# A decoder step on one core: main products that read and write from the last column to the first, with every second column of a slab as weights

## The chip, the cores and the metric

The kernel runs on one core of a Trainium2 chip. The metric is the time of one execution on the device, in microseconds; lower is better. TensorE multiplies: a product first loads a block of 128 x 128 weights (LDWEIGHTS) and then streams the columns of the moving operand through it (MATMUL), and the sums are written to PSUM. VectorE (DVE), ScalarE (ACT) and GpSimd (POOL) do the elementwise work, and SyncE (SP) issues the DMAs.

## The reference

One layer of a decoder with three parallel branches, on 256 prompt tokens and 8 x 4 sample tokens, 288 in all, in float32:

```python
h = rms_norm(x, p['g_mix'])
proj = h @ p['w_in']
u_lin, u_gate, q_sb, k_sb, v_sb, q_mem, gate_logits = jnp.split(proj, SPLIT_POINTS, axis=-1)
...                                   # y_conv: GLU, causal depthwise conv, LayerNorm, swish, projection
...                                   # y_sb: stick-breaking attention over paged keys and values
...                                   # y_mem: softmax attention into 256 memory tokens
gates = jax.nn.sigmoid((gate_logits + p['b_gate']).astype(jnp.float32)).astype(x.dtype)
merged = gates[:, :, 0] * y_conv + gates[:, :, 1] * y_sb + gates[:, :, 2] * y_mem
x = x + merged @ p['w_o']
h2 = rms_norm(x, p['g_mlp'])
x = x + jnp.square(jax.nn.relu(h2 @ p['w_up'])) @ p['w_down']
```

The model is 2048 wide and the MLP 8192. The large products (`w_in`, the three branch projections, `w_o`, `w_up`, `w_down`) hold nearly all of the arithmetic. The outputs are also the new keys and values, the last rows of the convolution's input, and the memory's keys and values.

## The kernel before

**Layout.** Activations lie with the features on the 128 partitions and the 288 tokens along the columns, so one product of a 128 x 128 block of weights with a tile of 288 columns gives 128 output features of all tokens. Weights are the loaded (stationary) operand, activations the moving one.

**Slabs.** All weights stand in one array `wall` of 504 slabs, each 128 partitions x 1024 words, put in order of use on the host in `_layout`. A main slab holds 8 blocks of 128 columns next to each other: `put` lays down the blocks of 1024 input rows for one tile of 128 outputs; `put_pair` lays 4 times two adjacent output tiles; `put_rows` lays two pieces of 512 columns. The first 16 slabs are for the memory's keys and values (L541), where the slab is the moving operand; the other 488 are weights of main products.

**Two parts for each number.** Each slab comes by DMA into a "wr" tile. ScalarE (L305) rounds it to float32r, the high part "wh", and VectorE (L316) takes the difference, the low part "wl". Activations are kept as a high and a low part as well. A product with full precision is three products: high weights with the high and with the low activation, and low weights with the high activation. So each main slab feeds 24 products. The tiles of the parts have small leads ahead of their data: weights of main slabs begin 5 words into their tile (`SHIFT`), the activations 4 or 36 words into theirs (`AHEAD`, `HOME`), 320 words apart (`APART`).

**The products.** `chunk` (L486 to L488) issues a list of products into one PSUM accumulation. `products` makes the list from one slab, the 16 with high weights first and then the 8 with low weights, in pieces of 6; `main_tile` does two slabs (2048 input rows) into one bank of PSUM and passes the sum on. `conv_products` does the first four tiles of `w_in` with its own list, and calls `chunk` too. The other matrix products (attention, sums of squares, transposes) issue their own instructions at other lines.

**Order.** The order of instructions on each engine is written by a planner (`Order`): each job is a generator that yields what it needs next (engine, estimated time, flags, buffers), and the planner always takes the one that can start first. A main product is entered with the estimate `MM` = 0.131 us.

Of the kernel before, what the change touches and what calls it, by code (L numbers as in the profile page):

```python
# [14 lines left out]
P = 128  # L15
D_MODEL = 2048
KT = D_MODEL // P
# [19 lines left out]
N_SLABS = 504  # L37
# [37 lines left out]
class Order:  # L75
# [15 lines left out]
    def add(self, gen, rank, at=None):  # L91
        job = Job(gen, rank, self.now.ready if at is None and self.now else at or 0.0)
        self.jobs.append(job)
        was, self.now = self.now, job
        self.step(job)
        self.now = was
# [10 lines left out]
    def give(self, pool, n=1):  # L107
        self.pools[pool] += [self.now.ready] * n
# [57 lines left out]
def pe(us, *flags, **take):  # L166
    return Ask("PE", us, flags, **take)
# [16 lines left out]
def tile_decoder_step(ctx: ExitStack, tc: tile.TileContext, xT, memT, wall, cvec, kmat, ptab,  # L184
                      kpool, vpool, mkc, mvc, hist,
                      yT, oK, oV, oCp, oCs, oMK, oMV):
    nc = tc.nc
# [24 lines left out]
    def bank(p):  # L212
        return tl(p, [P, 512])
# [107 lines left out]
    def start_slab(s):  # L321
        at_slab[:] = [s, order.now.ready]
# [10 lines left out]
    hm, hx = [None] * KT, [None] * KT  # L333
# [149 lines left out]
        done(rm_done)  # L483


    def chunk(ps, todo, first, last):  # L486
        for i, (w, a) in enumerate(todo):
            nc.tensor.matmul(ps, w, a, start=(first and i == 0), stop=(last and i == len(todo) - 1))  # L488

    slab_no = [0]  # L490
    FULL = [k * P for k in range(8)]
# [2 lines left out]
    def products(ps, uses, acts, first=True, last=True, n=T):  # L494

        s = slab_no[0] - 1
        sl = slabs[s]
        high = [(sl.h, c, a, x) for c, a in zip(uses, acts) for x in (0, 1)]
        low = [(sl.l, c, a, 0) for c, a in zip(uses, acts)]
        todo = high + low  # L500
        for i in range(0, len(todo), STEP):
            part = todo[i:i + STEP]
            yield pe(len(part) * MM, *sl.split, *{a.flag for _, _, a, _ in part})
            if i == 0 and first:
                start_slab(s)
            chunk(ps, [(w[:, c:c + P], a.l if x else a.h) for w, c, a, x in part],
                  first and i == 0, last and i + STEP >= len(todo))

    def main_tile(acts, evac, rank=1.0, n_slabs=2):
        yield pe(0.0, pm=1)  # L510
        ps = bank("pm")[:, :T]
        for i in range(n_slabs):
            slab_no[0] += 1
            yield from products(ps, FULL, acts[8 * i:8 * i + 8], i == 0, i == n_slabs - 1)
            give("w")
        add(evac(ps), rank)
# [33 lines left out]
    def conv_products(evacs):  # L550

        s0 = slab_no[0]
        slab_no[0] += KT // 2
        yield pe(0.0, pa=2)
        ps = [bank("pa")[:, :T], bank("pa")[:, :T]]
        lead = 3
        turns = [(k2, o) for k2 in range(lead) for o in (0, 1)] + [(k2, o) for k2 in range(lead) for o in (2, 3)]
        turns += [(k2, o) for k2 in range(lead, KT // 2) for o in range(4)]
        for k2, o in turns:
            s = s0 + k2  # L560
            sl = slabs[s]
            if len(ps) <= o:
                yield pe(0.0, pm=1)
                ps.append(bank("pm")[:, :T])
            todo = []
            for i in range(2):
                w = slice(i * 512 + o * P, i * 512 + (o + 1) * P)
                todo += [(sl.h, w, "h", 2 * k2 + i), (sl.h, w, "l", 2 * k2 + i)]
            for i in range(2):
                todo.append((sl.l, slice(i * 512 + o * P, i * 512 + (o + 1) * P), "h", 2 * k2 + i))  # L570
            yield pe(6 * MM, *sl.split, hx_in[2 * k2], hx_in[2 * k2 + 1])
            if o == 0:
                start_slab(s)
            chunk(ps[o], [(w[:, c], getattr(hx[k], x)) for w, c, x, k in todo], k2 == 0, k2 == KT // 2 - 1)
            if k2 == KT // 2 - 1:
                add(evacs[o](ps[o]), 1.0 + 0.01 * o)
            if o == 3:
                give("w")
        for k in range(KT):
            hx[k].flag = hx_in[k]  # L580
# [806 lines left out]
    def branch_products(br, acts):  # L1387
        for j0 in range(0, KT, 4):
            for j in range(j0, j0 + 4):
                yield from main_tile(hx, gate(br, j))  # L1390
            for j in range(j0, j0 + 4):
                if br == 1:
                    yield from main_tile(acts, branch(br, j), 1.0, 1)
                    continue
                yield pe(0.0, pm=1)
                ps = bank("pm")[:, :T]
                if j % 2 == 0:
                    slab_no[0] += 1
                yield from products(ps, [k * 2 * P + (j % 2) * P for k in range(4)], acts)
                if j % 2:  # L1400
                    give("w")
                add(branch(br, j)(ps), 1.0)
# [10 lines left out]
    def main():  # L1413
        yield from warm_up()
        yield from mem_products()
        yield from conv_products([evac_lin(0, "pa"), evac_gat(0, "pa"), evac_lin(1, "pm"), evac_gat(1, "pm")])
        for j in range(2, CT):
            yield from main_tile(hx, evac_lin(j, "pm"))
# [62 lines left out]
def _layout(inp):  # L1481
    import numpy as np

    a = {k: np.asarray(v) for k, v in inp.items()}
# [8 lines left out]
    x = np.concatenate([a["x_prompt"][0], a["x_sample"].reshape(NS, D_MODEL)], 0)  # L1493

    wall = np.empty((N_SLABS, P, SLAB), np.float32)
    at = [0]

    def put(w, j, r0=0, rows=D_MODEL):
        for half in range(rows // 1024):
            blk = w[r0 + half * 1024:r0 + (half + 1) * 1024, j * P:(j + 1) * P]  # L1500
            wall[at[0]].reshape(P, 8, P)[:] = blk.reshape(8, P, P).transpose(1, 0, 2)
            at[0] += 1
# [40 lines left out]
    for c in range(4):  # L1543
        for f in range(KT):
            put(a["w_up"][0], c * KT + f)
        for j in range(KT):
            put(a["w_down"][0], j, c * D_MODEL)
    assert at[0] == N_SLABS

    cvec = np.zeros((P, NCV), np.float32)  # L1550
    cvec[:, C_GMIX:C_GMIX + KT] = cols(a["g_mix"][0])
# [15 lines left out]
    i = np.arange(P)  # L1567
# [3 lines left out]
    r, c = i[:, None] % NS, np.arange(NS)[None, :]  # L1571
# [49 lines left out]
```

## Time and profile before

| | |
|---|---|
| time, median of 3 runs | 1634.39 us (1634.28 to 1634.63) |
| span of the profiled execution | 1632.5 us |
| the median less that span | 1.9 us |
| TensorE busy | 1627.7 us, 12,786 products |
| weight loads busy | 1610.3 us, 12,786 loads |
| DVE, ACT, POOL busy | 992.1, 739.3, 139.1 us |
| read from memory | 297.05 MB, 186 GB/s over the span with what is written |

For the profiled execution the span, from its first to its last instruction, is what is recorded as its own time. Products are pipelined: the duration of one goes from its issue to the drained end and overlaps the next, so the busy time of TensorE doesn't tell what a product costs; the distance from one start to the next does. Weight loads (PEld) overlap the products.

### The profile page before, as it was taken

Reading aid. Unit: us, or ns where it says so; the run is one execution under the profiler, and the core shown is the slowest. Engines: PE = TensorE matmul, PEld = TensorE weight load, DVE = VectorE, ACT = ScalarE, POOL = GpSimd, SP = SyncE. Lnnn points to the kernel's source line nnn. Section 1 sums busy time; section 2 is a strip of 40 time slices with the busy share of each in tenths; the row PEclk is TensorE's granted clock in tenths of the full one; section 3 lists DMA queues with packets and bytes.
Section 4 is the critical chain, followed back from the end, with each engine's and each line's share of the span. In section 5 each row is a group of like instructions: output and inputs, shape, how many; then the busy total and the mean of one; then the engine's idle time right before and its main releaser. Section 6 shows DMA issues by size and latency. Waiting matters only on the chain.

```text
span 1632.5 us, 30962 instructions
## 1 busy us (share of the span) xinstructions
PE 1627.7 (100%) x12786; PEld 1610.3 (99%) x12786; DVE 992.1 (61%) x1471; ACT 739.3 (45%) x1070; POOL 139.1 (9%) x104
## 2 busy tenths in 40 slices
PE   9999999999999999999999999999999999999999
PEld 7999999999999999999999999999999999999999
DVE  8889888877677655565555544455445554455443
ACT  8746766644444534444443333333333333333332
POOL 0020000000000000001222200121001210022100
PEclk9999999999999999999999999999999999999999
DMA  9787465777755555546655555555555555555563
GB/s 339 217 186 251 153 209 189 248 257 252 254 166 169 163 179 167 174 153 212 191 176 168 169 168 168 169 169 174 165 173 170 168 170 169 168 168 168 180 194 99
DMA packets 107103, 305.39 MB, mean 187 GB/s; under 512 B 19922, under 2 KB 29522, under 8 KB 106962
## 3 DMA queue, kind: packets, MB, share of 16 engines
q1 hardware_dynamic: 106818, 303.39, 58.2%
q8 instruction: 100, 1.64, 0.4%
q14 instruction: 41, 0.34, 0.1%
q10 hardware_dynamic: 144, 0.02, 0.0%
HBM read 297.05 MB, written 6.32 MB: 186 GB/s over the span
## 4 chain that ended last, share of the span: by engine, by line
PE 99%; DMA 0%; SPq 0%; ACT 0%; DVE 0%; issue 0%
PE pm L488 93%; PE pm L541 3%; PE pa L488 1%; PE pl L1017 1%; PE pl L1190 0%; PE pa L854 0%; PE pa L855 0%; PE pa L853 0%; DMA wr<-in_wall 0%; PE pl L1033 0%; PE pa L827 0%; PE pa L1144 0%; PE pa L908 0%; PE pa L1141 0%; PE pa L1143 0%; PE pa L1107 0%
## 5 line engine op out<-in xcount | busy, mean ns | idle before, releaser
L305 ACT CAST wh<-wr 128x1024 fp32r<-128x1024 f32 (+1 forms) x520 | 530.3, 1022 | 648.1 <-PE pm L488 597.0
L488 PE MATMUL pm<-a,wh 128*128 128x288 f32 x5184 | 739.1, 293 | 0.0
L316 DVE TENSOR_TENSOR wl<-wr,wh 128x1024 fp32r<-128x1024 f32 (+1 forms) x520 | 617.2, 1190 | 195.2 <-ACT wh L305 190.5
L488 PEld LDWEIGHTS pm<-a,wh 128*128 128x128 f32 x5184 | 696.7, 188 | 1.3 <-issue 1.2
L488 PE MATMUL pm<-a,wl 128*128 128x288 f32 x2592 | 397.0, 292 | 0.0
L488 PEld LDWEIGHTS pm<-a,wl 128*128 128x128 f32 x2592 | 358.4, 188 | 0.0
L488 PE MATMUL pm<-k,wh 128*128 128x288 f32 x2160 | 306.7, 292 | 0.0
L488 PEld LDWEIGHTS pm<-k,wh 128*128 128x128 f32 x2160 | 290.2, 188 | 0.0
L488 PE MATMUL pm<-k,wl 128*128 128x288 f32 x1120 | 171.6, 292 | 0.0
L488 PEld LDWEIGHTS pm<-k,wl 128*128 128x128 f32 x1120 | 155.1, 188 | 0.0
L1346 POOL TENSOR_TENSOR t<-t 128x288 f32<-128x288 f32 x64 | 96.7, 1511 | 599.5 <-DVE t L1343 599.5
L1360 DVE TENSOR_TENSOR a<-a,pm 128x288 f32<-128x288 f32 x64 | 29.0, 454 | 122.4 <-PE pm L488 122.4
L1343 DVE SCALAR_TENSOR_TENSOR t<-pm,rx 128x288 f32<-128x288 f32 x64 | 29.2, 457 | 90.4 <-PE pm L488 90.4
L1349 ACT CAST k<-t 128x288 fp32r<-128x288 f32 x56 | 24.1, 433 | 115.6 <-POOL t L1346 115.6
L1262 DVE TENSOR_TENSOR t<-pm,rx 128x288 f32<-128x288 f32 x48 | 22.0, 458 | 71.5 <-PE pm L488 71.5
L488 PE MATMUL pm<-s,wh 128*128 128x288 f32 x400 | 65.1, 292 | 0.0
L719 DVE SCALAR_TENSOR_TENSOR a<-a,cv,a 128x256 f32<-128x256 f32 x120 | 57.5, 480 | 1.4
L1332 POOL TENSOR_TENSOR t<-t,t 128x288 f32<-128x288 f32 x15 | 21.6, 1441 | 419.3 <-ACT t L1329 419.3
L488 PEld LDWEIGHTS pm<-s,wh 128*128 128x128 f32 x400 | 56.6, 188 | 0.0
L1351 DVE TENSOR_TENSOR k<-t,k 128x288 fp32r<-128x288 f32 x52 | 23.8, 458 | 51.1 <-ACT k L1349 51.1
L541 PE MATMUL pm<-wh,a 128*128 128x512 f32 x128 | 34.6, 391 | 0.2 <-ACT wh L305 0.2
L488 PE MATMUL pm<-s,wl 128*128 128x288 f32 x160 | 33.8, 292 | 0.0
(212 smaller groups left out, 784.4 us busy)
## 6 DMA issues: line engine op xcount, KB each, us to landing
wr<-in_wall SPq DMA_DIRECT2D x488, 512.0 KB, 3.6
wr<-in_wall SPq DMA_DIRECT2D x32, 256.0 KB, 4.8
k<-in_kpool SPq DMA_DIRECT2D x32, 256.0 KB, 5.9
k<-in_vpool SPq DMA_DIRECT2D x32, 256.0 KB, 5.8
k<-in_mkc SPq DMA_DIRECT2D x8, 512.0 KB, 10.2
k<-in_mvc SPq DMA_DIRECT2D x8, 512.0 KB, 6.5
t<-in_xT SPq DMA_DIRECT2D x16, 144.0 KB, 3.7
out_yT<-a SPq DMA_DIRECT2D x16, 144.0 KB, 1.9
```

The source lines that it names most:

```text
L305: nc.scalar.copy(sl.h[:, c], sl.raw[:, c])
L316: nc.vector.tensor_sub(sl.l[:, c], sl.raw[:, c], sl.h[:, c].bitcast(F32))
L488: nc.tensor.matmul(ps, w, a, start=(first and i == 0), stop=(last and i == len(todo) - 1))
L541: nc.tensor.matmul(ps[m], y[:, m * P:(m + 1) * P], z[:, w], start=(k == 0 and j < 2), stop=(k == KT - 1 and j in (4, 5)))
L719: nc.vector.scalar_tensor_tensor(c[:, :NP], up[:, k:k + NP], w, c[:, :NP], op0=ALU.mult, op1=ALU.add)
L1262: nc.vector.tensor_mul(g, ps, rx)
L1332: nc.gpsimd.tensor_add(sq_sum[0], sq_sum[0], res[0])
L1343: nc.vector.scalar_tensor_tensor(r, ps, 0.0, r2, op0=ALU.max, op1=ALU.mult)
L1346: nc.gpsimd.tensor_mul(r, r, r)
L1349: nc.scalar.copy(a.h, r)
L1351: nc.vector.tensor_sub(a.l, r, a.h.bitcast(F32))
L1360: nc.vector.tensor_add(x1[j], x1[j], ps)
```

## The change

In `chunk`, the moving operand is read from its last column to its first, and the sums are written to PSUM from the last column to the first, so that each sum lands where it did. The weights of a block are no longer 128 adjacent words of the slab but every second word of a pair of blocks (256 words): `block` gives the first, third, fifth ... word for the even block of the pair and the second, fourth ... for the odd one. The host lays the slabs out to match, from slab 16 on. The 16 memory slabs and all other matrix products are as before.

```diff
+    def block(w, c):
+
+        pair = w[:, c // (2 * P) * 2 * P:(c // (2 * P) + 1) * 2 * P]
+        return pair.rearrange("p (c two) -> p two c", two=2)[:, c // P % 2]
+
     def chunk(ps, todo, first, last):
         for i, (w, a) in enumerate(todo):
-            nc.tensor.matmul(ps, w, a, start=(first and i == 0), stop=(last and i == len(todo) - 1))
+            nc.tensor.matmul(ps[:, ::-1], w, a[:, ::-1], start=(first and i == 0), stop=(last and i == len(todo) - 1))
...
-            chunk(ps, [(w[:, c:c + P], a.l if x else a.h) for w, c, a, x in part],
+            chunk(ps, [(block(w, c), a.l if x else a.h) for w, c, a, x in part],
                   first and i == 0, last and i + STEP >= len(todo))
...
-            chunk(ps[o], [(w[:, c], getattr(hx[k], x)) for w, c, x, k in todo], k2 == 0, k2 == KT // 2 - 1)
+            chunk(ps[o], [(block(w, c.start), getattr(hx[k], x)) for w, c, x, k in todo], k2 == 0, k2 == KT // 2 - 1)
...
     assert at[0] == N_SLABS
+    for s in range(KT, N_SLABS):
+        v = wall[s].reshape(P, 4, P, 2)
+        v[:] = wall[s].reshape(P, 4, 2, P).transpose(0, 1, 3, 2).copy()
```

## The prediction

> **What bounds the kernel now.** I read the busy shares of the page first, then its chain that ended last, then the TensorE clock row.
>
> ```profile
> PE 1627.7 (100%) x12786; PEld 1610.3 (99%) x12786; DVE 992.1 (61%) x1471; ACT 739.3 (45%) x1070; POOL 139.1 (9%) x104
> ...
> PEclk9999999999999999999999999999999999999999
> ...
> PE 99%; DMA 0%; SPq 0%; ACT 0%; DVE 0%; issue 0%
> PE pm L488 93%; PE pm L541 3%; PE pa L488 1%; PE pl L1017 1%; PE pl L1190 0%; PE pa L854 0%; PE pa L855 0%; PE pa L853 0%; DMA wr<-in_wall 0%; PE pl L1033 0%; PE pa L827 0%; PE pa L1144 0%; PE pa L908 0%; PE pa L1141 0%; PE pa L1143 0%; PE pa L1107 0%
> ```
>
> TensorE is never idle for long, its clock is not cut, and 93 + 1 hundredths of the span are the products of L488, the only instructions of the program that the diff touches. So the change is worth what it does to the time from one L488 product to the next, and nothing else. How many there are, the instructions of that line tell (forms of the tiles that they read):
>
> ```profile
> L488 PE MATMUL pm<-a,wh x5184: 289/292/401, 54.0 to 1528.1; 128*128 128x288 f32 x200
> L488 PE MATMUL pm<-a,wl x2592: 289/292/383, 54.6 to 1529.2; 128*128 128x288 f32 x200
> L488 PE MATMUL pm<-k,wh x2160: 290/290/294, 730.3 to 1627.3; 128*128 128x288 f32 x197
> L488 PE MATMUL pm<-k,wl x1120: 290/292/294, 732.4 to 1628.7; 128*128 128x288 f32 x187
> L488 PE MATMUL pm<-s,wh x400: 290/294/294, 734.8 to 1628.0; 128*128 128x288 f32 x134
> L488 PE MATMUL pm<-s,wl x160: 290/290/294, 736.3 to 1629.0; 128*128 128x288 f32 x160
> L488 PE MATMUL pa<-a,wh x64: 290/292/382, 48.9 to 72.8; 128*128 128x288 f32 x64
> L488 PE MATMUL pa<-a,wl x32: 290/293/298, 49.4 to 73.1; 128*128 128x288 f32 x32
> ```
>
> The sum of the counts is 11,712. The duration of one (292 ns) is from its issue to its drained end and overlaps the next, so it is not what one costs. The cost is the distance of starts, which the chain in order of time gives, since it merges unbroken stretches (start, length, what, count):
>
> ```profile
> 541.70 297.18 PE pm L488 x2286
> 839.15 790.15 PE pm L488 x6078
> ```
>
> 790.15 us over 6078 products is 130.0 ns each, and 297.18 over 2286 is 130.0 too. So 11,712 x 130.0 ns = 1522.6 us of the 1632.5 us span are set by this one number. The rest, about 110 us, is the memory products of L541, the attention and convolution products, and the edges; the change leaves it alone. The profiled execution spans 1632.5 us; the median of the runs is 1634.39, so 1.9 us lie around the span, and I add them to every span below.
>
> **What of the 130 ns is streaming.** Products of other widths are priced in the same way, in the timeline of TensorE (start, length, what, count):
>
> ```profile
> 40.75 1.07 PE L541 MATMUL pm<-wh,a 128*128 128x512 f32 x4
> 41.65 0.61 PE L541 MATMUL pm<-wl,a 128*128 128x512 f32 x2
> 42.11 1.07 PE L541 MATMUL pm<-wh,a 128*128 128x512 f32 x4
> ...
> 128.80 0.28 PE L853 MATMUL pa<-a,a 128*128 128x256 f32 x1
> 128.92 0.28 PE L854 MATMUL pa<-a,a 128*128 128x256 f32 x1
> 129.03 0.28 PE L855 MATMUL pa<-a,a 128*128 128x256 f32 x1
> 129.16 0.28 PE L853 MATMUL pa<-a,a 128*128 128x256 f32 x1
> 129.28 0.28 PE L854 MATMUL pa<-a,a 128*128 128x256 f32 x1
> 129.40 0.28 PE L855 MATMUL pa<-a,a 128*128 128x256 f32 x1
> 129.51 2.25 PE L488 MATMUL pm<-a,wh 128*128 128x288 f32 x16
> ```
>
> Six products of 512 columns take 42.11 - 40.75 = 1.36 us, 226.7 ns each. Six of 256 columns take 129.51 - 128.80 = 0.71 us, 118.3 ns each. So a further column costs (226.7 - 118.3) / 256 = 0.423 ns, and 118.3 - 256 x 0.423 = 10 ns of each product are no streaming. A product of 288 columns streams for 288 x 0.423 = 121.9 ns, and 8.1 of the 130.0 ns are extra. With the slope between 288 and 512 columns instead, (226.7 - 130.0) / 224 = 0.432, streaming is 124.3 ns and 5.7 ns are extra. So 5.7 to 8.1 ns of each main product can be won at most: 67 to 95 us in all.
>
> Is that extra fixed? Two rows say that it depends on where the operands lie. By the line through 256 and 512 columns, 288 columns would cost 121.9 + 10 = 131.9 ns; those products read tiles without the leads AHEAD and SHIFT, and the main products, which have them, cost 130.0. And after the sum of squares, whose moving tile (a "t" tile) has no lead either, the next main product starts later than 130:
>
> ```profile
> 132.64 0.30 PE L827 MATMUL pa<-t,ones_r 128*128 128x288 f32 x1
> 132.78 2.26 PE L488 MATMUL pm<-a,wh 128*128 128x288 f32 x16
> ```
>
> That is 0.14 us for the same 288 columns on an engine with nothing to wait for (to a hundredth, so a weak witness alone). During each product the weights of the next are read from the same memory. I take the extra to be, mostly, these two reads getting in each other's way.
>
> [...]
>
> **The change part by part.** The number of products, of weight loads, of DMAs and of their bytes stays as it is, and so do the casts (L305) and subtractions (L316), which handle whole slabs; the shuffle of the slabs is done on the host, outside the time. The 16 memory slabs keep their layout. No wait is added, and the planner's order is the same, since MM and the asks are the same. Cost of all that: 0.
>
> *Moving columns last to first* (a[:, ::-1]): the same 288 adjacent words of 4 bytes, from the other end. No row shows such a read. [...] *Sums written last to first* (ps[:, ::-1]): the same words of the bank; no row shows it. Nearest is the forward write, 0; I take 0, and as an upper bound I keep one extra more, 8.1 ns.
>
> *Weights from every second column*: one load now walks over 1,024 bytes of a partition instead of 512. What a load costs by itself is seen where the products are short (weight loads, start and length):
>
> ```profile
> 176.10 0.19 PEld L1143 LDWEIGHTS pa<-s,ones_r 128*128 128x128 f32 x1
> 176.21 0.19 PEld L1144 LDWEIGHTS pa<-s,tri_r 128*128 128x128 f32 x1
> 176.32 0.36 PEld L488 LDWEIGHTS pm<-a,wh 128*128 128x128 f32 x2
> ```
>
> Loads follow each other at 0.11 us for 128 columns, 0.86 ns a column. So a load hides under a product of 0.130 us with 0.020 us to spare: it may become 18% longer for nothing. Bounds: 0 if a load at a step of two costs what it does now; 0.22 - 0.13 = +0.09 us for each product if it takes twice as long. I take 0. [...]
>
> *Both together*: now the product walks 4 bytes in 0.423 ns, 9.5 bytes/ns, and the load 4 bytes in 0.86 ns, 4.7 bytes/ns. [...] With a step of two the load walks 8 bytes in 0.86 ns, 9.3 bytes/ns: the same speed as the product, within the accuracy of the rows. If both also walk the same way, their distance stays what it is at the start, and a collision that holds one of them up shifts it out of the way of the next. Then most of the extra goes. The diff turns the product's way round; which way the load walks through its tile no row shows. Here I choose: the same way. Of the 5.7 to 8.1 ns I take 6.0, near the lower end, because some turn-around between products will remain, which these rows can't separate. Sum: 11,712 x 6.0 ns = 70.3 us; span 1632.5 - 70.3 = 1562.2; with 1.9, **1564.1 us**, at 124.0 ns a product.
>
> What would be late next: a slab feeds 24 products, 3.12 us now and 2.98 then. The stretches (PE, PEld, DVE, ACT, POOL busy; clock; DMA share) of the early and the late part:
>
> ```profile
> 200.00:300.00 100.00, 100.00 (x871) 99.24 (x870) 84.42 (x166) 66.58 (x135) 0.96 (x1) 1.00 0.64 225
> 1100.00:1200.00 100.00, 100.00 (x772) 100.00 (x771) 48.09 (x55) 35.61 (x38) 8.67 (x6) 1.00 0.54 170
> ```
>
> Late, DVE at 48% and ACT at 36% have room for a pace 5% higher. Early, DVE at 84% would go to some 88%; I cost this at nothing. If that cover is gone, the gain of the products outside the two long stretches is lost: 11,712 less 8,364 are 3,348, at 6.0 ns 20 us.
>
> **The rivals.** [...]
>
> *B: the load itself becomes the bound.* It decides once a load at a step of two lasts over 0.130 us. At twice the time, 0.22, the sum is 11,712 x 0.09 = +1054 us, 2688 us. [...]
>
> *C: nothing changes.* The extra is a turn-around inside TensorE, or the mirrored read and the mirrored write come to the engine as what they were, and the step of two hides in the 0.020 us. For it: the extra hardly varies, 130.0 in both long stretches. Against: the 1.9 ns and the 0.14 us. Time: 1634.4.
>
> **How the numbers follow.** Forecast 0.60, A 0.26, C 0.08, B 0.06. A measurement of this kernel can tell about 0.2% from no change, 3.3 us, or 0.28 ns a product. So faster 0.60, same 0.08, slower 0.32. The forecast's own range is from the whole extra gone (1634.4 - 95 = 1539) to a third of it (2 ns, 23 us: 1611). The range of the whole must take in C and a good part of A: up to 1700, which leaves out B and about 0.08 of A at the top, and a few hundredths below 1539. So 1539 to 1700.
>
> **What would show it.** Right: the long unbroken stretch of L488 at about 124 ns a product, L541 still at 227, weight loads still 0.19 us from issue to end, DVE's late share up to about 50%. If the step of two slows the load, that duration grows, and above all its distance of starts. [...] Early waits of L488 on L316 or L305 would show that the supply eats part of the gain. Wrong altogether: a distance of 130.0 as before, or over it.

## The result: 44 us slower

The changed kernel takes 1678.89 us (median of 4 runs, 1678.87 to 1679.38), the kernel before 1634.51 us beside it: 44.4 us more, a ratio of 1.0272 (95% interval 1.0257 to 1.0286). The prediction was 1564.1 us; the measured time lies in the stated range, on the other side of no change.

The page of the changed kernel first (`chunk` now issues at L493, the memory products are L546):

```profile
span 1677.6 us, 30962 instructions
...
PE 1672.9 (100%) x12786; PEld 1655.3 (99%) x12786; DVE 993.3 (59%) x1471; ACT 740.2 (44%) x1070; POOL 139.2 (8%) x104
...
PEclk9999999999999999999999999999999999999999
```

The work of DVE, ACT and POOL is what it was, TensorE is still busy throughout at an uncut clock (1.0 granted), and the span is 45.1 us longer. Its chain in order of time (start, length, what, count) has the same unbroken stretches:

```profile
555.68 306.32 PE pm L493 x2286
862.27 812.09 PE pm L493 x6078
```

812.09 us over 6078 products is 133.6 ns each, and 306.32 over 2286 is 134.0, where both were 130.0. 11,712 products at 3.6 to 4.0 ns more are 42 to 47 us: nearly the whole loss, beside about 1 us ahead of the first main product. The weight loads of that line (duration min/median/max in ns), before and after, show one thing more:

```profile
L488 PEld LDWEIGHTS pm<-a,wh x5184: 186/188/215, 53.9 to 1528.0; 128*128 128x128 f32 x200
```

```profile
L493 PEld LDWEIGHTS pm<-a,wh x5184: 192/196/220, 55.1 to 1570.2; 128*128 128x128 f32 x200
```

A weight load, from issue to end, had a median of 188 ns and now has 196. So the load did get longer, but by 8 ns, within the 20 ns that the prediction had found to spare.

### The profile page after: what moved, and what is told of

It is laid out like the page before. It is cut to its first block, busy times and chain, and to the rows that moved or that the text cites. A ratio compares the mean times of both kernels' runs of the same rounds, so it can differ in the third digit from the quotient of the medians.

```text
span 1677.6 us, 30962 instructions
## 1 busy us (share of the span) xinstructions
PE 1672.9 (100%) x12786; PEld 1655.3 (99%) x12786; DVE 993.3 (59%) x1471; ACT 740.2 (44%) x1070; POOL 139.2 (8%) x104
## 4 chain that ended last, share of the span: by engine, by line
PE 99%; DMA 0%; SPq 0%; ACT 0%; issue 0%; DVE 0%
PE pm L493 93%; PE pm L546 2%; PE pa L493 1%; PE pl L1022 1%; PE pl L1195 0%; DMA wr<-in_wall 0%; PE pa L859 0%; PE pa L860 0%; PE pa L858 0%; PE pl L1038 0%; PE pa L832 0%; PE pa L1149 0%; PE pa L913 0%; SPq L283 0%; PE pa L1146 0%; SPq L396 0%
## 5 line engine op out<-in xcount | busy, mean ns | idle before, releaser
L493 PE MATMUL pm<-a,wh 128*128 128x288 f32 x5184 | 756.2, 297 | 0.0
L493 PEld LDWEIGHTS pm<-a,wh 128*128 128x128 f32 x5184 | 717.2, 197 | 1.3 <-issue 1.2
L493 PE MATMUL pm<-a,wl 128*128 128x288 f32 x2592 | 410.7, 299 | 0.0
L493 PEld LDWEIGHTS pm<-a,wl 128*128 128x128 f32 x2592 | 371.3, 197 | 0.0
L493 PE MATMUL pm<-k,wh 128*128 128x288 f32 x2160 | 314.4, 297 | 0.0
L493 PEld LDWEIGHTS pm<-k,wh 128*128 128x128 f32 x2160 | 299.1, 197 | 0.0
L493 PE MATMUL pm<-k,wl 128*128 128x288 f32 x1120 | 177.1, 298 | 0.0
L493 PEld LDWEIGHTS pm<-k,wl 128*128 128x128 f32 x1120 | 159.9, 197 | 0.0
L493 PE MATMUL pm<-s,wh 128*128 128x288 f32 x400 | 65.5, 295 | 0.0
L493 PEld LDWEIGHTS pm<-s,wh 128*128 128x128 f32 x400 | 57.5, 195 | 0.0
L546 PE MATMUL pm<-wh,a 128*128 128x512 f32 x128 | 35.6, 399 | 0.1
L493 PE MATMUL pm<-s,wl 128*128 128x288 f32 x160 | 34.6, 298 | 0.0
```

Of the source, the lines that this page charges most:

```text
L493: nc.tensor.matmul(ps[:, ::-1], w, a[:, ::-1], start=(first and i == 0), stop=(last and i == len(todo) - 1))
L546: nc.tensor.matmul(ps[m], y[:, m * P:(m + 1) * P], z[:, w], start=(k == 0 and j < 2), stop=(k == KT - 1 and j in (4, 5)))
```

## The experiments

Three theories stood at the start: the step of two costs by itself (1), the two reads get in each other's way and how both walk decides (2), the mirrored write costs (3). The kernels that change form or lead along the way were each executed once; their rows are read as distances of starts, time over products.

**Each half alone.** Mirror only: the kernel before, with

```diff
-            nc.tensor.matmul(ps, w, a, start=...
+            nc.tensor.matmul(ps[:, ::-1], w, a[:, ::-1], start=...
```

> The mirrored read and write alone, weights adjacent as before. [...] Theory 2 (the collisions of the two reads depend on how both walk, so each half of the change has an effect of its own): off 130.0 by 1 ns or more either way, below 1623 or above 1646 us. Theory 3 (the mirrored write to PSUM costs): 133.6 ns, 1679 us, the whole loss.

Step only: the changed kernel, with

```diff
-            nc.tensor.matmul(ps[:, ::-1], w, a[:, ::-1], start=...
+            nc.tensor.matmul(ps, w, a, start=...
```

> Weights from every second column alone, columns read and written forward. Theory 1 (the step of two alone costs): 133.6 ns a main product and 1679 us, the whole loss. Theory 2 (both walks matter): another number than the changed kernel's, 1 ns or more away from 133.6, and from 130.0 as well. Theory 3 (the mirrored write): 130.0 ns, 1634 us.

Measured: mirror only 1672.98 us (ratio 1.0230, 1.0213 to 1.0247), step only 1672.72 us (1.0229, 1.0212 to 1.0246), against 1635.05. The chains, mirror only first, then step only:

```profile
857.61 810.40 PE pm L488 x6078
```

```profile
857.33 810.41 PE pm L493 x6078
```

Each half alone costs 133.3 ns a product, 38 us, and both together only 6 us more than either. Theories 1 and 3 each make one half free, so both fall as the whole story. Of theory 2's numbers the mirror's came true; the step's 133.3 is only 0.3 ns from the changed kernel's 133.6, not the 1 ns that it had asked for.

**All forms side by side.** A kernel that changes the form along the MLP: read forward or mirrored, write forward or mirrored, step 1, 2, 4 or 8, lead of the slabs 5 or 0 words, each form at a source line of its own.

```diff
+FORMS = [(1, 1, 1, 5), (1, 1, 1, 5), (1, -1, 1, 5), (-1, 1, 1, 5), ...]    # read, write, step, lead
+def form_of(s):
+    return 0 if s < 248 else 1 + (s - 248) // 16
```

> As the kernel before up to the MLP; in the MLP 16 forms of main product in a row, 8 output tiles (384 products) each, each at a line of its own: read forward or mirrored, write forward or mirrored, step of weights 1 or 2 (all eight, two of each four leave the tokens mirrored in those tiles, so the output isn't the reference's), then steps 4 and 8 forward and mirrored, then steps 1 and 2 forward and mirrored with the slabs' lead at 0 in place of 5 words. [...] Theory 2: the read's direction and the lead change it by 1 ns or more at either step; the write's doesn't. Theory 3: the forms with a mirrored write are the slow ones, at any step.

Its chain, one line for each form (the last two, step 2 at lead 0, are left out; both are at 133.3 to 133.4 ns):

```profile
840.02 41.34 PE pm L518 x318
881.36 49.92 PE pm L519 x384
931.28 51.19 PE pm L520 x384
982.48 51.20 PE pm L521 x384
1033.67 51.20 PE pm L522 x384
1084.87 51.20 PE pm L523 x384
1136.07 51.30 PE pm L524 x384
1187.37 51.30 PE pm L525 x384
1238.67 90.02 PE pm L526 x384
1328.70 89.82 PE pm L527 x384
1418.52 92.69 PE pm L528 x384
1511.21 93.20 PE pm L529 x384
1604.41 50.35 PE pm L530 x384
1654.76 50.35 PE pm L531 x384
...
```

L518 to L521 are step 1: forward read, then with a mirrored write (41.34 over 318 and 49.92 over 384, both 130.0 ns), then the mirrored read with either write (both 133.3). L522 to L525 are the same four at step 2: 133.3, 133.3, 133.6, 133.6. So the direction of the write costs nothing, at either step: theory 3 is gone. L526 to L529 are steps 4 and 8: 234 to 243 ns, about twice the 0.11 us at which loads follow each other at step 1. There the load seems to be the bound: its medians go from 188 ns at step 1 and 196 at step 2 to 329 to 340 at steps 4 and 8. So there is a cliff, between steps 2 and 4. L530 and L531, step 1 with the lead at 0, are 131.1 forward and 131.1 mirrored: the same mirrored read that costs 133.3 at lead 5. The place matters as much as the direction, as theory 2 has it.

**The place, swept.** The changed form in the MLP with leads of 0 to 31 words, each at its own line (L534 is lead 0, L565 lead 31):

```diff
+FORMS = [(1, 1, 1, 5)] + [(-1, -1, 2, k) for k in range(32)]
```

> As the kernel before up to the MLP; in the MLP the changed form (mirrored read and write, step 2) with the slabs' lead at 0, 1, ... 31 words in place of 5, 4 output tiles (192 products) each, each at a line of its own. [...] Theory 2 (the two reads keep a fixed distance, and the distance decides): the distance of starts swings with the lead, with a period of 4 or of 32 words, by 3 ns or more, and some leads come below 130.0 (down to 124) where the two reads miss each other. Theory 3 (the write): 133.6 everywhere.

The chain from lead 1 on; the rows left out at the end have the same length as that of lead 7 to 0.02 us:

```profile
857.02 25.73 PE pm L535 x192
882.74 25.60 PE pm L536 x192
908.34 25.71 PE pm L537 x192
934.06 26.36 PE pm L538 x192
960.42 25.86 PE pm L539 x192
986.28 25.17 PE pm L540 x192
1011.46 25.17 PE pm L541 x192
...
```

Leads 1 to 5 cost 134.0, 133.3, 133.9, 137.3 and 134.7 ns; from 6 on all are at 25.17 / 192 = 131.1. So the place decides, as theory 2 has it; but no lead is below 130.0, and there is no period in it. Had the pace locked at lead 6 by chance? The next kernel goes the other way, from lead 41 (L544) down to 0 (L585), 3 tiles each.

> The changed form in the MLP again, with the lead falling from 41 to 0 words, 3 output tiles (144 products) each, each at a line of its own. Theory P (the place decides, with a period of 32 words, 128 bytes): 131.1 ns at 6 to 31 words as in the rising sweep, and the leads 32 to 37 as dear as 0 to 5 (133.3 to 137.3 ns), 38 to 41 at 131.1. Theory H (history: the pace locks into a state and keeps it, and the rising sweep happened to lock at lead 6): the dear leads are others than 0 to 5, or 32 to 41 have no such stretch, and what comes after a change of state stays in it.

```profile
1491.74 18.89 PE pm L579 x144
1510.63 19.24 PE pm L580 x144
1529.87 19.77 PE pm L581 x144
1549.65 19.28 PE pm L582 x144
```

Lead 6 (L579) is at 131.2 ns (and all from 41 down to 7 at 131.1, 18.88 for 144), leads 5, 4, 3 at 133.6, 137.3, 133.9. The same leads are dear in both orders, so it is not history, though how dear is not always the same: lead 0 had 133.4 rising and has 136.7 here. Nor is there a period of 32 words, since 32 to 37 are cheap. Theory P was right on the place and wrong on the period; of theory H only the sign came true, that 32 to 37 are not dear. Next: is it the lead in the slab's tile, or the distance from the moving columns? All moving tiles 8 words further on:

```diff
-AHEAD, HOME = 4, 36
+AHEAD, HOME = 12, 44
```

> The rising sweep of the changed form (leads 0 to 31, 4 output tiles each) with all moving tiles 8 words further on (AHEAD 12, HOME 44 for 4, 36). Theory D (what counts is the distance from the moving columns to the weights): the dear leads move up by 8: 8 to 13 words cost 133.3 to 137.3 ns, 14 to 31 131.1, the highest at 12. Theory L (the lead in the slab's tile alone counts): dear at 0 to 5 as before, 131.1 from 6 on.

Leads 11 to 14 (L545 to L548):

```profile
1131.47 25.71 PE pm L545 x192
1157.19 26.36 PE pm L546 x192
1183.55 25.86 PE pm L547 x192
1209.42 25.17 PE pm L548 x192
```

133.9, 137.3, 134.7 and 131.1 ns: what was found at leads 3 to 6, to the hundredth of a microsecond, now stands at 11 to 14. The distance from the moving columns to the weights decides; the lead by itself does not. The band reaches down to lead 0 in this kernel too (25.46 to 26.24 us for 192), so it is 14 words wide at least.

The products ahead of the MLP, in the form of before at lead 5, changed as well in this kernel:

```profile
799.98 48.54 PE pm L533 x364
```

133.4 ns, where the rising sweep, with the columns in their old place, has 130.0 for the same form (31.20 us for 240). So the place of the columns counts for the form of before too, and the kernel before stands at a cheap one.

**The other forms, swept in the same way.** Forward at step 1 (the kernel before), mirrored at step 1, forward at step 2.

> The form of the kernel before (forward, step 1) in the MLP, with the lead at 0, 1, ... 31 words, 4 output tiles (192 products) each. Theory P: 130.0 at lead 5 and 131.1 at lead 0 as measured, and among the rest a band of leads that costs 133 ns or more, since now the two reads walk against each other and where they start decides where they meet; the best stays at 130.0 or above if the extra of 10 ns is a fixed turn-around, and comes below 129 if it was collisions. Theory H: two or three levels in an order that has nothing to do with the lead.

> Mirrored read and write, step 1, with the lead at 0 to 31 words, 4 output tiles each. Theory P: 133.3 at lead 5 and 131.1 at lead 0 as measured; a band of dear leads, and elsewhere 130 to 131.1. If the two reads walk the same way here, but at speeds of 2 to 1, the dear band is narrower than half of the leads. Theory H: no order by lead.

> Forward read and write, step 2, with the lead at 0 to 31 words, 4 output tiles each. Theory P: 133.3 at leads 0 and 5 as measured. If the load walks last to first, the reads now pass each other at the full speed of both, so they meet at any lead and 133.3 or so is found at all 32. If the load walks first to last, a wide band of leads at 131.1 is found, as for the mirrored form. Theory H: no order by lead.

Forward, step 1, leads 3 to 7: the worst of the 32 and some of the best:

```profile
906.74 25.91 PE pm L537 x192
932.65 25.59 PE pm L538 x192
958.25 24.96 PE pm L539 x192
983.21 25.61 PE pm L540 x192
1008.81 24.97 PE pm L541 x192
```

135.0, 133.3, 130.0, 133.4, 130.1 ns. Nine of the 32 leads are at 130.0 or within 0.2 of it, lead 5 among them, and none is below; the others lie between 131.1 and 135.0 in no order that I can read. Nor is it the lead alone: lead 0 gave 130.1 here and 131.1 in the kernel of all forms. Mirrored at step 1 runs from 131.1 to 133.4, no band either. So at step 1 the band that theory P asked for is missing, the levels stand in no order by lead, as theory H had it, and what sets them stays open. Forward at step 2, the cheapest and the dearest (leads 17 and 16), and lead 0's neighbour:

```profile
856.75 25.60 PE pm L535 x192
```

```profile
1240.91 25.96 PE pm L550 x192
1266.88 25.50 PE pm L551 x192
```

133.3, 135.2 and 132.8 ns; most leads are at 133.3 and none at 131.1. That is what e8's expectation gives for a load that walks last to first: forward, the two reads pass each other at any lead; mirrored, they keep their distance, and a wide range of leads is free of trouble. It fits the sweeps at step 2. At step 1 it is not borne out: there, e7 asked for one band of dear leads, and found none. No run shows the load's direction itself.

**Is the rest of the extra collisions at all?** The products narrowed to 288, 286, 284, 282, 280, 272, 256, 224 columns, in the form of before (L519 to L526) and in the changed form at lead 16 (L527 to L534):

```diff
+            n = T if first and i == 0 else WIDTHS[form_of(s)]
+            RUNS[form_of(s)](ps[:, :n], w, a[:, :n], ...)
```

> As the kernel before up to the MLP; in the MLP all products of an output tile but its first use only the first 288, 286, 284, 282, 280, 272, 256, 224 columns (8 tiles each, each at a line of its own), first in the form of before (forward, step 1, lead 5), then in the changed form with the lead at 16, so the sums of the last columns lack most of their terms. Theory F (about 10 ns of each product are a fixed turn-around, and only 0 to 7 ns more are collisions): the distance of starts falls with the width at 0.42 ns a column and keeps some 10 ns over it: about 117 at 256 columns, 103 to 105 at 224, unless the load's 0.11 us becomes the bound (then 108 to 110). Theory Q (a product costs a whole number of steps of 3.33 ns, since the levels 130.0, 133.3 and their means are all that was seen): the same, but in steps: 130.0 holds for several widths and then drops to 126.7. My forecast's theory (the extra is collisions of the two reads over the length of the load): the changed form at lead 16 has less extra than the form of before at small widths.

```profile
880.85 50.77 PE pm L520 x384
931.62 49.48 PE pm L521 x384
981.11 49.54 PE pm L522 x384
1030.64 49.93 PE pm L523 x384
1080.57 47.86 PE pm L524 x384
1128.43 45.38 PE pm L525 x384
1173.81 43.03 PE pm L526 x384
```

132.2, 128.9, 129.0, 130.0, 124.6, 118.2 and 112.1 ns for 286 to 224 columns (the first product of each 48 keeps its 288, which adds 0.6 ns at most). With 0.423 ns a column, 8.1 ns are extra at 288, 8.7 to 11.6 from 286 down to 256, where it is 9.9, as between the products of other lines (10). The changed form at lead 16, at 272, 256 and 224 columns:

```profile
1468.16 47.84 PE pm L532 x384
1516.00 45.33 PE pm L533 x384
1561.33 45.33 PE pm L534 x384
```

At 272 columns it costs 124.6 ns, as in the form of before. At 256 and at 224 it costs the same 118.0: a pace that does not change with the width is not that of streaming, so I take it to be the load's, at a step of two, and the 112.1 at 224 columns to be the load's at step 1. So wherever the load does not set the pace the extra is there, and at 272 columns it is as large in the changed form as in the form of before, where the forecast's theory asked for less: theory F. What the extra is, no run shows.

That 286 columns cost more than 288 is more than a price for each column can give. Theory Q, which asked for whole steps of 3.33 ns, did not come true as it stood: neither form stays at 130.0 over several widths and then drops to 126.7. Nor is a level such as 131.1 a mix of products at 130.0 and 133.3: in the trace of the next experiment 11,565 of the 11,637 distances from one main product to the next are 130, 131 or 132 ns. The reason for the levels is open.

**The changed kernel at a cheap place.**

```diff
-SHIFT = 5
+SHIFT = 16
```

> The changed kernel with SHIFT 16 for 5, the lead being 16 words in all main slabs. Theory D and theory L: 131.1 ns a main product, 11,712 x 1.1 ns = 13 us over the kernel before, 1647 to 1649 us; the other 31 us of the loss were the place alone. If the MLP's sweep does not hold for the rest of the kernel: 1650 to 1679 us.

Measured: 1647.83 us (1647.73 to 1647.95), ratio to before 1.0078 (1.0061 to 1.0095).

```profile
845.96 796.91 PE pm L493 x6078
```

131.1 ns a product, as both theories of its expectation had it. So of the 44 us, some 32 go when the slabs move by 11 words, and 13 stay. None of the swept forms or places is below 130.0 ns at 288 columns, so the runs point to no version that beats the kernel before.

## Why the prediction was wrong

**What bounds the kernel: right.** Nearly the whole change of time is the distance of starts of the main products times 11,712; nothing else moved by more than about 1 us, and the early wait for slabs that it feared did not show.

**The step of two: right that the load does not bind, wrong that it is free.** 0 was taken, within 0.020 us to spare. At the widths where I take the load to set the pace it is 112.1 ns at step 1 and 118.0 at step 2, so by these runs 12 of the 130 ns are still to spare; about twice the time, as rival B has it, came at steps 4 and 8 (234 to 243 ns a product). But the step alone made the product 3.3 ns dearer at lead 5 (133.3, 38 us), and 132.8 is the lowest of its sweep.

**The mirrored write: right**, 130.0 with it and without.

**The mirrored read alone: wrong.** The forecast's sum takes it as free, which no run shows for every place; the runs showed 3.3 ns more at lead 5 (133.3 against 130.0) and nothing at lead 0 (131.1 both ways). So its price hangs on the place, which the prediction left out.

**Both together: here the forecast failed.** The step that failed is "I take the extra to be, mostly, these two reads getting in each other's way". It stood in the sum as -6.0 ns a product, 70.3 us; measured are +3.6 to +4.0 ns and +44.4 us. An effect of the two operands' places is real: with mirrored columns and a step of two, their distance moves a product between 131.1 and 137.3 ns, and the price stays fixed over 36 leads in a row, which fits the choice "the same way". But in no run does it take anything off the 130.0; it only adds. Some 8 ns or more over streaming (at 0.423 ns a column) stay in every form and place at 288 columns, and at the smaller widths until the load sets the pace, so the kernel before, at lead 5, had nothing of it that these runs could win back.

The two signs that I read as its share don't carry that. The 131.9 was a line drawn through 256 and 512 columns, and the widths run is off such a line with no place changed (132.2 at 286 columns). The 0.14 us is real (133 to 138 ns in the trace after 14 of the 18 such products, longer after the rest), but 3 to 8 ns at one change of operands say nothing of how much is left to win.

**"A collision that holds one of them up shifts it out of the way of the next": wrong.** In the band of distances below lead 6 nothing shifts out of the way: 133 to 137 ns as long as the form runs. The prediction also never asked at which distance the two reads would lock. SHIFT 5 is the last lead of that band; 2.5 of the 3.6 ns are that, and 1.1 remain at the best place. Why the changed form has 131.1 there and not 130.0 is open; its load is 7 to 8 ns longer at step 2, but the mirrored read at step 1, with the load at 188 ns, has 131.1 at its best leads too.

**The rivals.** A, the slower rival with 0.26, had the right sign, and the measured time lies in the part of the range that was kept for it. No run shows reads that collide more often; what the runs showed in place of that is an extra that stayed, plus 31.6 us of a bad distance and 12.8 that are open. C's reason, a turn-around inside TensorE that no order of addresses changes, fits what the runs show of the extra, without being shown; the prediction gave it 0.08 for its claim on the time. The places of the operands do count for the time: at lead 12, mirrored and at a step of two, moving the columns 8 words on took a product from 131.1 to 137.3 ns.

## What to carry to other kernels

Take a cost over streaming that hardly varies as fixed until a run shows that it moves: vary one width or one offset before it goes into a sum as something to win. Where the weights of the next product are read during this one, as here, take offsets, directions and steps of the two operands as one setting, not three (131.1 to 137.3 ns in these runs at one form and 32 leads); change one and sweep the offset again, and it can be swept in one run, with each value at a source line of its own. Here a step of two words in float32 weights cost the load little (118.0 against 112.1 ns, where I take the load to set the pace) and the product 3.3 ns at lead 5 (133.3 against 130.0); at a step of four a product took 234 ns, and the load seems to be the bound.

## What the runs showed of the hardware that I had not expected

In the form of before, 286 columns cost more (132.2 ns) than 288 (130.0), and moving all moving tiles by 8 words took its main products from 130.0 to 133.4. The direction of the write to PSUM made no difference (130.0 both ways). With mirrored columns and a step of two, one word of lead decided: 133.6 to 134.7 ns at 5, 131.1 from 6 to 41. At a step of four or eight words a product took 234 to 243 ns, a little over twice the 0.11 us at which loads follow each other at step 1.
